# Pacing the late modulation steps of a diffusion transformer block behind its weight loads

## The chip, the cores and the metric

The kernel runs on one core of a Trainium2 chip. The metric is the device time of one execution in microseconds. Five engines work side by side, each through its own instructions in order: TensorE (PE) multiplies, VectorE (DVE) and ScalarE (ACT) do the elementwise work, GpSimd (POOL) and SyncE (SP) here only issue transfers.

## The reference

One block of a diffusion transformer over 256 tokens `x` and 256 context tokens, width 2048, all in float32:

```
mod = silu(c) @ w_ada + b_ada                 # six vectors of 2048: shift, scale, gate, twice
px  = modulate(x, norm1_g, mod 0, mod 1) @ w_in    # and the context likewise
rec = gated linear recurrence, both directions, 8 heads of 128, chunks of 64
att = windowed attention, 8 query heads on 2 key heads, with the context's keys and a sink
mix = (sigmoid(g_r) * (rec @ w_rec) + sigmoid(g_a) * (att @ w_att)) @ w_out
x_mid = x + mod 2 * mix
new_x = x_mid + mod 5 * conv_ffn(modulate(x_mid, norm2_g, mod 3, mod 4))
```

Vectors 0 and 1 are needed at once. The later ones, 2, 4, 3 and 5, are needed behind the merge, and it is their computation that is moved.

## The kernel before

Nearly all the time is matrix products over weights that are read once, 512 KB at a time, in one stream `wst`. A *weight load* (`Stream.load`, L104 to L112) is a transfer from SP's queue into one of four `raw` buffers, a copy on ACT rounded to float32r (`whi`, L109) and a subtraction on DVE that leaves the remainder (`wlo`, L110); three buffers each. Loads are numbered here by their subtraction, 1 to 498. Products are made of two or three matmuls (`hi*hi`, `hi*lo`, `lo*hi`). `duo` (L371) makes two output tiles at once: per load 8 matmuls of 512 columns and 8 of 256. `fold` (L398) empties an output bank: a copy on ACT, an addition on DVE (L400). Five banks serve these outputs (`bankm`), three the small products (`banks`).

The order of stages, with their loads: the first modulation vectors and the first products (1 to 16), q of the recurrence (17 to 32), eight heads of the recurrence with v and the attention's k and v among them (33 to 74), the attention's q (75 to 90), gate g (91 to 106), the recurrent merge gate (107 to 138), the merge (139 to 202; 8 loads for a pair of tiles), the output projection (203 to 234), the FFN. The small products of the recurrence and the attention wait in a list `tasks`; `tick` puts one of them between two pieces of a stage's products.

The late modulation vectors are made on the side, by a generator `ada_steps` (L320). A vector is done in two halves of 16 *steps*; a step issues a transfer of 512 KB from POOL's queue into one of two buffers `araw` (L330) and an accumulation on DVE (L333 the first, L335 the others). After 16 steps come two empty calls, and then one that transposes the sum on PE (L343) and reduces it on DVE (L344): 19 calls for a half, 152 in all. `ada(n)` (L355) makes the next n calls. It is called by hand after pieces of work, 1 to 4 calls together.

A scheduler sets the order on each engine. It goes by the place in the program, moved by hand: a weight load stands up to 60 places early (`LEAD`), a call of `ada` 60 late (`LAG`) and not ahead of the latest load's subtraction. Behind the merge the input is read again into `xm` by two loads of 1 MB (L765, L766), as soon as the recurrence's buffer is free.

Of the kernel before, what the change touches and what calls it, by code (L numbers as in the profile page):

```python
# [50 lines left out]
def block_kernel(ctx, tc, xct, prm, cst, ada2, wst, out):  # L51
# [46 lines left out]
    class Stream:  # L98
        def __init__(self):
            self.half = 0  # L100
            self.pos = 8
            self.hi = self.lo = None

        def load(self, n=8):  # L104
            with tc.high_priority(offset=min(LEAD, max(0, tc.tile_snap_priority() - base[0]))):
                raw, hi, lo = [strm.tile([P, 1024], dt, name=nm, bufs=b)[:, 0:n * P]
                               for nm, dt, b in (("raw", F32, 4), ("whi", F32R, 3), ("wlo", F32R, 3))]
                nc.sync.dma_start(raw, wst[self.half, :, 0:n * P])
                S.copy(hi, raw)  # L109
                self.last = V.tensor_tensor(lo, raw, hi.bitcast(F32), op=ALU.subtract)  # L110
            self.half += 1
            self.hi, self.lo, self.pos = hi, lo, 0  # L112

        def load_raw(self, into):
            with tc.high_priority(offset=min(LEAD, max(0, tc.tile_snap_priority() - base[0]))):
# [10 lines left out]
    st = Stream()  # L126
# [488 lines left out]
    for h in range(H):  # L615
        if h == 4:
            bs = [bank() for _ in range(4)]
            natural(bs, range(4))
            ada(4)
            for tt in range(4):  # L620
                S.copy(vn[:, tt, 512:1024], bs[tt])
        if h == 6:
            bs = [bank() for _ in range(4)]
            natural(bs, range(4))
            ada(4)
            kv_evac(bs)
        for d in range(2):
            if 2 * h + d < 3:
                o = early_f[2 * h + d]
            else:  # L630
                o = bank()
                tform_all(o)
            hgrn_a(h, d, o)
            ada(0 if h > 5 else 2 if h else 1)
        hgrn_q(h)
        tasks += [lambda h=h: hgrn_e(h - 1), lambda h=h: hgrn_b(h), lambda h=h: hgrn_c(h), lambda h=h: hgrn_d(h)]
        ada(1)
        if h == 0:
            q_heads(4)
# [8 lines left out]
    split(kTh, kTl, kT.rearrange("p k (s t) -> p k s t", s=2))  # L648
    split(vah, val, va.rearrange("p (a b) t -> p a b t", a=2))

    bs = [bank() for _ in range(2)]
    for g in range(2):
        if g:
            bs = [bank() for _ in range(2)]
        natural(bs, range(2))
        ada(1)
        if not g:
            assert not tasks
            gr = big.tile([P, KT, T], F32, name="gr", tag="v")
# [54 lines left out]
    for kv in range(2):  # L714
        for blk in range(2):
            tasks += [lambda kv=kv, blk=blk, i=i: att_scores(kv, blk, i) for i in range(4)] + [lambda: None]
            tasks += [lambda kv=kv, blk=blk, k=k: (att_trans(kv, blk, k), att_trans(kv, blk, k + 1)) for k in (0, 2)]
            tasks += [lambda kv=kv, blk=blk: att_out(kv, blk)]
    for h in range(0, H, 2):
        for i, o in enumerate(duo((xx, xx))):  # L720
            fold(qo[:, 0, h + i, :], o)
        ada(2)

    def y_rec(p):
        hs = slice(2 * p, 2 * p + 2)
# [4 lines left out]
    for j in range(0, KT, 2):  # L730
        for i, o in enumerate(duo((xx, xx))):
            fold(gr[:, j + i, :], o)
        if YR <= j < YR + 4:
            assert not tasks
            y_rec(j - YR)
            y_rec(j - YR + 1)
            ada(2)
        else:
            ada(2 + 2 * (j >= 8))
    for j in range(0, KT, 4):  # L740
        S.activation(gr[:, j:j + 4, :], gr[:, j:j + 4, :], AF.Sigmoid)

# [2 lines left out]
    for j in range(0, KT, 2):  # L745
# [6 lines left out]
        for i, ga in enumerate(gas):  # L752
# [4 lines left out]
            V.tensor_tensor(ga[:, 0:T], ga[:, 0:T], ga[:, T:], op=ALU.mult)  # L757
            V.tensor_tensor(ga[:, 0:T], ga[:, 0:T], gr[:, j + i, :], op=ALU.add)
            split(yb[:, j + i, 1, :], yb[:, j + i, 0, :], ga[:, 0:T])
            ada(0 if j + i == 15 else 3 if i else 2)  # L760

    with tc.issue_after(sig.ins):
        S.preload_act_table_set("natural_log_exp_and_others")
    xm = big.tile([P, KT, T], F32, name="xm", tag="qo")
# [24 lines left out]
    for j in range(0, KT, 2):  # L789
        for i, o in enumerate(duo((yb, yb))):  # L790
            with tc.high_priority(offset=RUSH if j == KT - 2 else 0):
                mid_evac(j + i, o)
        if 2 <= j < 8:
            ada(2 if j < 6 else 1)
        if j == 10:
            split(pre[:, 0, :, T:], pre[:, 1, :, T:], sh2[:, :, None].broadcast_to([P, KT, 2]))

# [229 lines left out]
```

## Time and profile before

| | us |
|---|---|
| runs shown: median, lowest, highest | 1717.17, 1711.70, 1721.25 |
| profiled execution, its own time | 1713.84 |
| its span (first to last instruction) | 1712.0 |
| moved, mean rate | 371.84 MB, 217 GB/s |

The page gives each engine's busy time and a chain of what ended last. PE is nearly always busy, but a busy PE need not be at its peak, since the ends of matmuls are modelled. How many matmuls begin in a slice of fixed length tells more, within one stage. Times in the rows are from the span's start.

### The profile page before, as it was taken

The numbers are of one execution on the slowest core, as the hardware profiler recorded it, in microseconds if no ns is written. First come the engines' busy times: TensorE is split into PE (matmuls) and PEld (weight loads), VectorE is DVE, ScalarE is ACT, GpSimd is POOL, SyncE is SP. The second block draws the span as 40 slices with busy tenths as digits, with TensorE's granted clock in tenths as the row PEclk, the third lists the DMA queues.
The fourth block names the chain that finished last, engine by engine and source line by source line (L and its number), as shares of the span: only waits on it lengthen the run. The fifth ranks groups of instructions, "written<-read, shape, count | busy, mean of one in ns | idle before, by whom it ended". The sixth has DMA issues, their size and how long they took to land.

```text
span 1712.0 us, 24746 instructions
## 1 busy us (share of the span) xinstructions
PE 1683.9 (98%) x9438; PEld 1424.6 (83%) x9438; DVE 1202.3 (70%) x1890; ACT 837.2 (49%) x1278; POOL 68.7 (4%) x132
## 2 busy tenths in 40 slices
PE   7999999999999999999999999999999999999999
PEld 2668888888888888888888988888888888888887
DVE  4438876675779787787878788787766655666565
ACT  4237453342646664444454565555555434554332
POOL 0000100100000001010100000000000000000000
PEclk9999999999999999999999999999999999999999
DMA  9986734524346568787866577677655555555564
GB/s 377 385 328 225 259 120 150 198 88 152 104 149 220 173 228 299 253 288 248 301 227 235 184 233 258 222 258 262 219 185 186 190 190 186 193 188 187 193 198 148
DMA packets 104008, 371.84 MB, mean 217 GB/s; under 512 B 11344, under 2 KB 13776, under 8 KB 103888
## 3 DMA queue, kind: packets, MB, share of 16 engines
q1 hardware_dynamic: 85456, 303.14, 50.9%
q0 software_dynamic: 18432, 67.12, 12.3%
q8 instruction: 74, 1.21, 0.3%
q14 instruction: 46, 0.38, 0.1%
HBM read 368.11 MB, written 2.10 MB: 216 GB/s over the span
## 4 chain that ended last, share of the span: by engine, by line
PE 85%; DMA 5%; DVE 5%; issue 3%; ACT 1%; SPq 0%; POOL 0%; DVEq 0%; POOLq 0%; ACTq 0%
PE bankm L68 78%; DMA araw<-in_ada_dram 5%; PE banks L68 5%; DVE wlo L110 1%; DVE acc L335 1%; DMA ringq<-in_wst_dram 1%; DVE xraw L230 0%; ACT whi L109 0%; PE banks L343 0%; PE banks L535 0%; PE banks L701 0%; PE banks L527 0%; SPq L116 0%; ACT t L220 0%; PE banks L536 0%
## 5 line engine op out<-in xcount | busy, mean ns | idle before, releaser
L68 PE MATMUL bankm<-hl,whi 128*128 128x512 f32 (+1 forms) x3392 | 1056.4, 393 | 2.3 <-DVE t L400 2.3
L110 DVE TENSOR_TENSOR wlo<-raw,whi 128x1024 fp32r<-128x1024 f32 x498 | 606.1, 1219 | 297.3 <-ACT whi L109 295.9
L109 ACT CAST whi<-raw 128x1024 fp32r<-128x1024 f32 x498 | 520.3, 1045 | 554.1 <-PE bankm L68 488.2
L68 PEld LDWEIGHTS bankm<-hl,wlo 128*128 128x128 f32 x3104 | 583.8, 188 | 138.6 <-DVE wlo L110 7.1
L68 PE MATMUL bankm<-hl,wlo 128*128 128x256 f32 (+2 forms) x3104 | 665.4, 287 | 4.8 <-DVE wlo L110 4.8
L68 PEld LDWEIGHTS bankm<-hl,whi 128*128 128x128 f32 x3392 | 535.1, 189 | 22.8 <-DVE t L400 3.0
L335 DVE SCALAR_TENSOR_TENSOR acc<-araw,csil,acc 128x1024 f32<-128x1024 f32 x120 | 153.7, 1281 | 37.8 <-DMA araw<-in_ada_dram 37.3
L68 PE MATMUL bankm<-whi,hl 128*128 128x512 f32 x512 | 165.5, 396 | 4.3 <-ACT hl L206 3.3
L68 PEld LDWEIGHTS bankm<-whi,hl 128*128 128x128 f32 x512 | 95.8, 188 | 26.6 <-ACT hl L206 5.5
L330 POOL DMA_DIRECT2D araw<-in_ada_dram x128 | 68.5, 535 | 1144.3 <-DVE acc L335 659.6
L68 PE MATMUL bankm<-wlo,hl 128*128 128x512 f32 x256 | 100.1, 391 | 0.0
L68 PE MATMUL bankm<-yb,whi 128*128 128x512 f32 x256 | 80.8, 397 | 0.0
L68 PE MATMUL bankm<-g,whi 128*128 128x512 f32 x256 | 80.4, 395 | 0.0
L68 PEld LDWEIGHTS bankm<-g,wlo 128*128 128x128 f32 x256 | 48.1, 188 | 11.4
L68 PEld LDWEIGHTS bankm<-yb,wlo 128*128 128x128 f32 x256 | 48.1, 188 | 11.3
L68 PEld LDWEIGHTS bankm<-wlo,hl 128*128 128x128 f32 x256 | 48.1, 188 | 9.5
L852 DVE SCALAR_TENSOR_TENSOR xm<-bankm,modv,xm 128x256 f32<-128x256 f32 x96 | 42.2, 480 | 18.4 <-PE bankm L68 18.3
L834 ACT ACTIVATE fs<-fs,prm 128x256 f32<-128x256 f32 x44 | 26.5, 602 | 55.9 <-DVE fs L400 55.9
L68 PE MATMUL bankm<-yb,wlo 128*128 128x256 f32 x256 | 50.6, 279 | 0.0
L68 PE MATMUL bankm<-g,wlo 128*128 128x256 f32 x256 | 50.3, 278 | 0.0
L195 DVE TENSOR_REDUCE tn<-banks 128x8 f32<-128x32 f32 x8 | 1.5, 192 | 64.7 <-ACT whi L109 51.4
L835 DVE SCALAR_TENSOR_TENSOR fs<-fs,prm,fs 128x255 f32<-128x255 f32 x44 | 21.3, 484 | 26.7 <-ACT fs L834 26.7
(216 smaller groups left out, 1227.5 us busy)
## 6 DMA issues: line engine op xcount, KB each, us to landing
raw<-in_wst_dram SPq DMA_DIRECT2D x490, 512.0 KB, 3.7
araw<-in_ada_dram POOLq DMA_DIRECT2D x128, 512.0 KB, 4.7
ringv<-in_wst_dram SPq DMA_DIRECT2D x24, 512.0 KB, 8.4
ringq<-in_wst_dram SPq DMA_DIRECT2D x20, 512.0 KB, 9.0
araw<-in_wst_dram SPq DMA_DIRECT2D x10, 512.0 KB, 9.3
xraw<-in_xct_dram SPq DMA_DIRECT2D x8, 512.0 KB, 10.2
raw<-in_wst_dram SPq DMA_DIRECT2D x8, 384.0 KB, 8.5
ringkT<-in_wst_dram SPq DMA_DIRECT2D x5, 512.0 KB, 10.1
```

What stands on the lines that cost most here:

```text
L68: return PE.matmul(o, l, r, start=start, stop=stop, skip_group_check=True)
L109: S.copy(hi, raw)
L110: self.last = V.tensor_tensor(lo, raw, hi.bitcast(F32), op=ALU.subtract)
L195: V.tensor_reduce(m8, aps.rearrange("p (q g c) -> p q c g", q=4, g=4)[:, :, 0:2, :], axis=AX.X, op=ALU.add)
L330: nc.gpsimd.dma_start(raw, ada2[idx])
L335: V.scalar_tensor_tensor(acc, raw, csil[:, kt, 0:1], acc, op0=ALU.mult, op1=ALU.add)
L834: S.activation(t, s, AF.Identity, bias=cb[:, f:f + 1], scale=cw[:, f, 1:2])
L835: V.scalar_tensor_tensor(t[:, 1:T], s[:, 0:T - 1], cw[:, f, 0:1], t[:, 1:T], op0=ALU.mult, op1=ALU.add)
L852: V.scalar_tensor_tensor(xm[:, j, :], o[:, T * i:T * i + T], gate2[:, j:j + 1], xm[:, j, :], op0=ALU.mult, op1=ALU.add)
```

## The change

`Stream` gets a rate, `pace`: calls of the generator for 16 loads. Each load adds it to a sum, and whenever the sum reaches 16 one call is made, right behind the load. The rate is 6 from the attention's q on (6 calls over 16 loads), 8 from gate g to the end of the merge (a call every second load), and 0 from there. The calls by hand in these stages go. Heads 6 and 7 of the recurrence get one call for each direction, where they had none, and the output projection two calls after each of four pairs, where it had 2, 2 and 1 after three. The description also names a return of the input in sixteen loads, one per merged tile; the two loads of the input (L769 now) stand as they were.

```diff
@@ Stream.__init__, Stream.load
+            self.pace = self.due = 0
...
             self.hi, self.lo, self.pos = hi, lo, 0
+
+            self.due += self.pace
+            if self.due >= 16:
+                self.due -= 16
+                ada()
@@ heads of the recurrence
             hgrn_a(h, d, o)
-            ada(0 if h > 5 else 2 if h else 1)
+            ada(1 if h > 5 or not h else 2)
@@ attention's q
+    st.pace = 6
     bs = [bank() for _ in range(2)]
...
         natural(bs, range(2))
-        ada(1)
@@ gate g
+    st.pace = 8
     for h in range(0, H, 2):
         for i, o in enumerate(duo((xx, xx))):
             fold(qo[:, 0, h + i, :], o)
-        ada(2)
@@ recurrent merge gate
             y_rec(j - YR + 1)
-            ada(2)
-        else:
-            ada(2 + 2 * (j >= 8))
@@ merge
             split(yb[:, j + i, 1, :], yb[:, j + i, 0, :], ga[:, 0:T])
-            ada(0 if j + i == 15 else 3 if i else 2)
-
+
+    st.pace = 0
@@ output projection
-        if 2 <= j < 8:
-            ada(2 if j < 6 else 1)
+        if 2 <= j < 10:
+            ada(2)
```

In the built order the lines from L115 on are 6 higher than before up to the attention, and 3 higher in the merge and behind it. Three places on DVE show what moves.

The first is the stretch around loads 126 to 135, the end of the recurrent merge gate, in which SP issues the two loads of the input. L335, now L341, is an accumulation. Before, and then with the change:

```order
L335 SCALAR_TENSOR_TENSOR acc<-araw,csil,acc 128x1024
L110 TENSOR_TENSOR wlo<-raw,whi 128x1024 x2
L400 TENSOR_TENSOR gr<-bankm,gr 128x256 x2
L110 TENSOR_TENSOR wlo<-raw,whi 128x1024
L335 SCALAR_TENSOR_TENSOR acc<-araw,csil,acc 128x1024 x2
L110 TENSOR_TENSOR wlo<-raw,whi 128x1024 x2
L335 SCALAR_TENSOR_TENSOR acc<-araw,csil,acc 128x1024 x2
L110 TENSOR_TENSOR wlo<-raw,whi 128x1024
```

```order
L111 TENSOR_TENSOR wlo<-raw,whi 128x1024 x2
L406 TENSOR_TENSOR gr<-bankm,gr 128x256 x2
L111 TENSOR_TENSOR wlo<-raw,whi 128x1024 x4
L406 TENSOR_TENSOR gr<-bankm,gr 128x256 x2
L111 TENSOR_TENSOR wlo<-raw,whi 128x1024 x2
L350 TENSOR_REDUCE modv<-banks 128x4 x2
L339 TENSOR_SCALAR acc<-araw,csil 128x1024
```

The accumulations that stood in twos between the subtractions are gone from here; the reduction of a finished half (L350) and the first accumulation of the next follow behind load 134.

The second is one pair of tiles of the merge, from load 152 on. L400, now L406, is the fold; L755, now L758, the product with the gate.

```order
L110 TENSOR_TENSOR wlo<-raw,whi 128x1024
L335 SCALAR_TENSOR_TENSOR acc<-araw,csil,acc 128x1024 x2
L110 TENSOR_TENSOR wlo<-raw,whi 128x1024
L400 TENSOR_TENSOR t<-bankm,t 128x256 x2
L110 TENSOR_TENSOR wlo<-raw,whi 128x1024
L335 SCALAR_TENSOR_TENSOR acc<-araw,csil,acc 128x1024 x2
L110 TENSOR_TENSOR wlo<-raw,whi 128x1024
L400 TENSOR_TENSOR t<-bankm,t 128x256
L755 TENSOR_TENSOR gr<-gr,t 128x256
```

```order
L341 SCALAR_TENSOR_TENSOR acc<-araw,csil,acc 128x1024
L111 TENSOR_TENSOR wlo<-raw,whi 128x1024
L406 TENSOR_TENSOR t<-bankm,t 128x256 x2
L111 TENSOR_TENSOR wlo<-raw,whi 128x1024
L341 SCALAR_TENSOR_TENSOR acc<-araw,csil,acc 128x1024
L111 TENSOR_TENSOR wlo<-raw,whi 128x1024
L406 TENSOR_TENSOR t<-bankm,t 128x256
L758 TENSOR_TENSOR gr<-gr,t 128x256
```

Two accumulations in a row have become single ones, two subtractions apart.

The third is the front of the attention, loads 96 to 98. L690, now L696, takes the maximum of a row of scores, the start of a softmax. Before, and with the change:

```order
L110 TENSOR_TENSOR wlo<-raw,whi 128x1024
L578 TENSOR_TENSOR gr<-gr,t 128x512
L400 TENSOR_TENSOR qo<-bankm,qo 128x256
L110 TENSOR_TENSOR wlo<-raw,whi 128x1024
L130 TENSOR_TENSOR ab<-banks,ab 128x4x128
L690 TENSOR_REDUCE tn<-banks 128x1 x2
```

```order
L111 TENSOR_TENSOR wlo<-raw,whi 128x1024
L584 TENSOR_TENSOR gr<-gr,t 128x512
L350 TENSOR_REDUCE modv<-banks 128x4 x2
L406 TENSOR_TENSOR qo<-bankm,qo 128x256
L136 TENSOR_TENSOR ab<-banks,ab 128x4x128
L696 TENSOR_REDUCE tn<-banks 128x1
```

Two reductions of a finished half stand here now; before they stood behind load 115.

## The prediction

> **What bounds the kernel now.** I read the page first, then TensorE (PE) in slices, then what released it in the slices that fall short.
>
> ```profile
> PE 1683.9 (98%) x9438; PEld 1424.6 (83%) x9438; DVE 1202.3 (70%) x1890; ACT 837.2 (49%) x1278; POOL 68.7 (4%) x132
> PE 85%; DMA 5%; DVE 5%; issue 3%; ACT 1%; SPq 0%; POOL 0%; DVEq 0%; POOLq 0%; ACTq 0%
> ```
>
> PE is the bound. Nothing in the change takes a matmul away, so all it can win is time in which PE falls behind, and that shows in how many matmuls a slice holds (in brackets), better than in busy time:
>
> ```profile
> core 0: us, PE busy (x) PEld busy (x) DVE busy (x) ACT busy (x) POOL busy (x), PEclk, DMA share, GB/s
> 660.00:680.00 20.00, 17.22 (x90) 14.59 (x90) 13.57 (x14) 6.92 (x9) 2.55 (x5) 0.91 0.99 366
> 680.00:700.00 20.00, 20.00 (x117) 17.43 (x116) 10.31 (x12) 9.84 (x13) 0.09 (x1) 1.00 0.67 229
> 720.00:740.00 20.00, 19.70 (x113) 16.91 (x111) 15.46 (x21) 9.80 (x15) 1.65 (x4) 1.00 0.84 278
> 740.00:760.00 20.00, 18.84 (x108) 16.49 (x109) 18.45 (x26) 10.45 (x17) 2.04 (x4) 1.00 0.84 278
> 820.00:840.00 20.00, 18.88 (x107) 15.75 (x106) 16.67 (x22) 9.45 (x16) 3.17 (x6) 1.00 0.89 310
> 860.00:880.00 20.00, 19.12 (x111) 16.37 (x110) 16.32 (x26) 11.59 (x19) 0.53 (x1) 1.00 0.72 246
> ```
>
> An undisturbed slice holds 117 matmuls, 20/117 = 0.171 us each. The other five lack 27, 4, 9, 10 and 6: 56 x 0.171 = **9.6 us**, of which 4.6 us in the first. All five lie where the change acts. What stopped PE, first in the merge, then in the first slice (VectorE, DVE, runs in order):
>
> ```profile
> 735.20 1.28 DVE L335 SCALAR_TENSOR_TENSOR acc<-araw,csil,acc 128x1024 f32<-128x1024 f32 x1 [1.98 <-DMA araw<-in_ada_dram]
> 738.35 1.28 DVE L335 SCALAR_TENSOR_TENSOR acc<-araw,csil,acc 128x1024 f32<-128x1024 f32 x1 [1.87 <-DMA araw<-in_ada_dram]
> 739.55 1.22 DVE L110 TENSOR_TENSOR wlo<-raw,whi 128x1024 fp32r<-128x1024 f32 x1
> 740.69 0.42 DVE L400 TENSOR_TENSOR t<-bankm,t 128x256 f32<-128x256 f32 x1
> DVE acc L335: 37.3, 32
> ```
>
> In a burst of steps the first two have their weights in the two buffers; the third's transfer starts only when the first step has freed its buffer. DVE then waits for it, and behind it stand the subtraction that makes PE's weights (L110) and the fold that empties PE's bank (L400). The last row is from the view of the transfer's line, under who waited for it: over the whole run DVE stood 37.3 us in 32 waits.
>
> ```profile
> 659.81 0.43 SPq L766 DMA_DIRECT2D xm<-in_xct_dram  x1
> 669.38 1.28 DVE L335 SCALAR_TENSOR_TENSOR acc<-araw,csil,acc 128x1024 f32<-128x1024 f32 x1 [1.20 <-DMA araw<-in_ada_dram]
> 673.42 1.28 DVE L335 SCALAR_TENSOR_TENSOR acc<-araw,csil,acc 128x1024 f32<-128x1024 f32 x1 [2.75 <-DMA araw<-in_ada_dram]
> 674.01 1.05 ACT L109 CAST whi<-raw 128x1024 fp32r<-128x1024 f32 x1 [5.10 <-DMA raw<-in_wst_dram]
> 674.62 1.22 DVE L110 TENSOR_TENSOR wlo<-raw,whi 128x1024 fp32r<-128x1024 f32 x1
> 672.00:676.00 4.00, 1.22 (x7) 1.00 0.87 348
> 676.00:680.00 4.00, 4.00 (x15) 0.57 0.96 318
> 680.00:684.00 4.00, 4.00 (x25) 1.00 0.90 292
> xm<-in_xct_dram SPq DMA_DIRECT2D x2, 1024.0 KB, 11.3
> ```
>
> The same burst, and with it the input's return, two loads of 1 MB (L766). The last three slices are PE alone: it stands 2.78 us, and then runs at a granted clock of 0.57, 15 matmuls instead of 25: 10 x 0.171 = 1.7 us more.
>
> The page "TensorE: Matmul & The Clock Gate" of the Trainium skill (Part 1, What's actually happening) lets the clock fall after an idle window of about 3.4 us; by it a gap of 2.78 us costs no clock, and the sum below would be 1.7 us smaller. The row shows the clock falling, and the measurement decides.
>
> **The change part by part.** The words name a return in sixteen loads; the diff has none, and the built order still has both 1 MB loads, now with one weight load between them instead of two. So only steps are moved. A step issues one 512 KB transfer from POOL's queue and one DVE instruction:
>
> ```profile
> L110 DVE TENSOR_TENSOR wlo<-raw,whi 128x1024 fp32r<-128x1024 f32 x498 | 606.1, 1219 | 297.3 <-ACT whi L109 295.9
> L335 DVE SCALAR_TENSOR_TENSOR acc<-araw,csil,acc 128x1024 f32<-128x1024 f32 x120 | 153.7, 1281 | 37.8 <-DMA araw<-in_ada_dram 37.3
> araw<-in_ada_dram POOLq DMA_DIRECT2D x128, 512.0 KB, 4.7
> DMA to landing us min/median/max: 3.7/4.7/7.8
> ```
>
> From heads 6 and 7 on the calls are, before and after: heads 2 and 6, attention's q 2 and 6, gate g 8 and 8, recurrent gate 20 and 16, merge 37 and 32, output projection 5 and 8, FFN 34 and 32: 108 both times.
>
> *The merge's bursts* (-5.0 us, four slices). A weight load is 16 matmuls, 2.74 us; a step every second load is one per 5.5 us. With two buffers a transfer starts two steps, 11 us, ahead of its use and lands in 4.7. So the waits go. DVE still has to fit: a pair of merged tiles is 8 loads, 21.9 us of PE; DVE has 8 x 1.22 + 14 small operations x 0.42 + 5 steps x 1.28 = 22.1 us before, and with 4 steps 20.8. It was at the brim and is now 5% under. I take all 5.0; the other end is half of it, if a step before a fold still holds a bank.
>
> *The input's return* (-4.6 us). By the order no accumulation stands between that of load 124 and the reduction behind load 134, since two empty calls and the transposes fall there. So DVE has nothing to wait for there, and the POOL queue brings almost nothing beside the 2 MB. What is late next is the raw weights themselves (5.10 us on the ACT row, which came after PE had already stopped). I take the 4.6 gone and charge what is left below; the other end is 2.3.
>
> *What is left* (+1.0 us). Behind the transposes at loads 135 and 172 the held-back steps catch up, about one per load: the third of these is due 5.5 us after the first, its weights 4.7 us after, at worst 7.8. Half a microsecond at each; ends 0 and 3.
>
> *Hgrn of head 7* (+0.9 us). A step now stands on DVE behind the subtraction of load 77, ahead of L467, in a chain on which PE waits already:
>
> ```profile
> 468.93 1.22 DVE L110 TENSOR_TENSOR wlo<-raw,whi 128x1024 fp32r<-128x1024 f32 x1
> 470.62 0.55 DVE L467 TENSOR_SCALAR hb<-hb,lb_t 128x512 f32<-128x512 f32 x1 [0.47 <-ACT hb L466]
> 475.84 0.42 DVE L485 TENSOR_TENSOR hb<-hb,qo 128x256 f32<-128x256 f32 x1
> PEld banks L68: 0.2, 1
> ```
>
> The last row, from the view of L485, is PE's weight load waiting for it. The step fills the 0.47 us of idle and pushes the chain by 1.28 - 0.6 = 0.7; L485 moves ahead of the next subtraction but behind other products, and what PE reads second comes later too. I take 0.9; ends 0 (the moved subtraction gives 1.2 back) and 1.8 (nothing absorbed, one more product).
>
> *The front of the attention* (+0.9, and -0.5 behind it). The order puts seven more accumulations ahead of load 88, ten ahead of load 116, and the two reductions of a finished vector half ahead of load 97 instead of 116.
>
> ```profile
> 480.00:500.00 20.00, 10.47 (x13) 1.00 0.51 161
> 500.00:520.00 20.00, 17.57 (x31) 1.00 0.58 185
> 540.00:560.00 20.00, 20.00 (x36) 1.00 0.74 234
> 550.04 0.48 DVE L696 TENSOR_SCALAR gr<-gr,tn 128x512 f32<-128x512 f32 x1
> 550.58 0.44 PE L701 MATMUL banks<-cst,gr 128*128 128x128 f32 x2
> 796.74 0.69 DVE L344 TENSOR_REDUCE modv<-banks 128x4 f32<-128x512 f32 x1 [0.42 <-PE banks L343]
> ```
>
> The early ones fall into idle time (9.5 us of it from 480 to 500, 2.4 from 500 to 520). Between 540 and 560 DVE has none, and PE's transposes start 0.06 us after the softmax row they read. What comes in ahead of that row: two reductions of 0.69 and 0.2 of small work, less the 0.5 by which an opening step is shorter than the one it replaces: 0.9 after rounding down for the overlap of neighbours. Ends 0 and 3 (if every step that is ahead there, three, counts). In return the same reductions leave the place near 604 where PE waited 0.2, and the fourth block starts with fewer steps ahead of it (0.3).
>
> *The rest* at nothing: the three added calls in the output projection lie where DVE still has 1.4 to 3.2 us of 20 free and PE loses none, and the two that leave the FFN were hidden there.
>
> ```profile
> 900.00:920.00 20.00, 20.00 (x119) 17.49 (x119) 16.77 (x30) 9.65 (x15) 0.53 (x1) 1.00 0.58 186
> 920.00:940.00 20.00, 20.00 (x117) 17.42 (x116) 18.58 (x30) 10.12 (x16) 1.58 (x3) 1.00 0.82 287
> ```
> If that cover were gone, three steps would cost 3.8 us.
>
> Sum: -5.0 - 4.6 + 1.0 + 0.9 + 0.9 - 0.5 = **-7.3 us**. The profiled execution took 1713.84 us (span 1712.0), so 1706.5 on its own scale; it lay 3.3 us below the median of 1717.17, and on the median's scale I get **1710**. The runs shown differ among themselves by 9.5 us, more than the gain.
>
> **The rivals.**
>
> *All of it and more:* the two losses do not appear, and the slower runs of before were slower through these same waits. For it: they hang on when transfers land. Against: PE's edge at 550. -9.6 - 0.5 with nothing lost gives 1707; the 3.3 us on top, 1704.
>
> *The first slice stays:* its stall belongs to the 2 MB, whose sixteen smaller loads are not in the code. For it: the raw weights landed 5.10 us late for ACT. Against: PE stopped on a subtraction behind an accumulation. Then -7.3 + 4.6 = -2.7, 1714.5.
>
> *Slower, DVE becomes the bound in the attention:* ten steps ahead at 1.28 and two reductions are 14.2 us of DVE where 480 to 560 has little idle. It decides from the point at which DVE, once behind, no longer catches up between the blocks. 14.2 - 9.6 = +4.6, and three gaps long enough to cost the clock 1.7 each make +9.7: 1727. Against: seven of the ten fall before 520.
>
> **How the numbers follow.** Forecast 50%, all of it 30%, first slice stays 12%, slower 8%. What this measurement can tell from no change is 0.5%, 8.6 us. A fifth of the forecast (its losses near their lower ends) and all of the second case are beyond it: 0.10 + 0.30 = 0.40 faster. Slower by that much are three quarters of the last, 0.06; the remaining 0.54 is within. The range goes from below 1704 to past 1714.5 with 3 us for the spread of medians: 1702.5 to 1718.
>
> **What would show it.** Right: DVE's wait for the accumulation's transfers falls from 37.3 us to under 20 (what is left lies before 480), the five slices hold 115 to 117 matmuls, the clock stays at 1.00 behind 660, and small new gaps of about 1 us appear near 476 (PE on L491) and 550 (PE on the softmax rows). Wrong: a slice between 500 and 650 that lacks more than 15 matmuls (DVE as bound), a gap of PE near 675 with the raw weights late (the input's return alone), or accumulations that still wait though spaced.

## The result

| | before | with the change |
|---|---|---|
| median, us | 1716.57 (6 runs) | 1705.74 (6 runs, 1704.42 to 1709.57) |
| profiled execution, its own time | 1713.84 | 1707.89 |
| its span | 1712.0 | 1706.1 |

The ratio is 0.9949, with an interval of 0.9932 to 0.9965: 8.8 us faster, within 6.0 to 11.7 us, and the 10.8 us between the two medians lie in it. In two later comparisons, each against its own runs of before, the same kernel had 0.9937 (0.9921 to 0.9953) and 0.9945 (0.9932 to 0.9957), at medians of 1704.51 and 1704.70 us.

The page of the changed kernel has these rows for the engines' busy time and for the chain of waits:

```profile
PE 1681.3 (99%) x9438; PEld 1425.0 (84%) x9438; DVE 1202.3 (70%) x1890; ACT 835.4 (49%) x1278; POOL 69.0 (4%) x132
PE 94%; DVE 3%; DMA 1%; issue 1%; ACT 1%; SPq 0%; DVEq 0%; ACTq 0%
```

PE's own share of the chain went from 85 to 94%; transfers fell from 5 to 1%. PE in slices (busy time, matmuls in brackets, granted clock, DMA share, GB/s), the five that fell short before:

```profile
660.00:680.00 20.00, 20.00 (x119) 1.00 0.77 257
720.00:740.00 20.00, 20.00 (x117) 1.00 0.87 291
740.00:760.00 20.00, 20.00 (x116) 1.00 0.86 277
820.00:840.00 20.00, 20.00 (x117) 1.00 0.85 281
860.00:880.00 20.00, 20.00 (x116) 1.00 0.72 244
```

All are full. The waits that end with a transfer of the accumulation's weights are next: first over the whole run, then from 480 to 1120 us alone (total us, times, longest).

```profile
DVE acc L341 <- DMA araw<-in_ada_dram: 20.7, 19, 2.9
...
DVE acc L341 <- DMA araw<-in_ada_dram: 4.2, 3, 1.8
```

Before, the same stretch had 18 of them:

```profile
DVE acc L335 <- DMA araw<-in_ada_dram: 22.0, 18, 2.8
```

On DVE's timeline, where PE had stood 2.78 us, no accumulation is left, and DVE waits for nothing but the copy on ACT:

```profile
671.44 1.23 DVE L111 TENSOR_TENSOR wlo<-raw,whi 128x1024 fp32r<-128x1024 f32 x1 [1.56 <-ACT whi L110]
...
674.23 1.23 DVE L111 TENSOR_TENSOR wlo<-raw,whi 128x1024 fp32r<-128x1024 f32 x1 [0.89 <-ACT whi L110]
677.06 1.23 DVE L111 TENSOR_TENSOR wlo<-raw,whi 128x1024 fp32r<-128x1024 f32 x1 [1.61 <-ACT whi L110]
```

**Where the time went, to the hundredth.** Every trace has the same 9438 matmuls, so the start of the n-th can be compared between traces. I took the starts of matmuls 1189, 2221, 2473, 3383, 3646, 4735 and 5195; the table gives the time to the first and then between neighbours, in us. The two bold columns are the ones in which the input's return and the merge's bursts lie.

| | to 1189: first products, first heads | to 2221: heads | to 2473: head 7 | to 3383: attention | **to 3646: recurrent gate, input's return** | **to 4735: merge** | to 5195 |
|---|---|---|---|---|---|---|---|
| before | 243.58 | 203.13 | 43.78 | 165.73 | **49.88** | **193.95** | 76.28 |
| the change | 246.99 | 203.12 | 43.93 | 165.66 | **45.27** | **189.21** | 76.28 |
| the change, second profile | 243.41 | 203.13 | 43.93 | 165.64 | **45.27** | **189.21** | 76.27 |
| the change, third profile | 245.21 | 203.13 | 43.93 | 165.59 | **45.27** | **189.21** | 76.27 |

Behind matmul 1189 the change wins 4.61 us at the input's return and 4.74 in the merge, wins 0.07 in the attention, and gives 0.15 back in head 7: -9.27 in all, the same in three executions to 0.1. The rest is before 1189, where the order of the instructions did not change: it took 242.8 to 247.0 us in the eleven profiles with that order (before, the change three times, and seven experiments). The profiled pair shows only -6.0 because this part went 3.4 us against the change. These rows of the changed kernel show it, DVE first, then PE:

```profile
208.95 1.28 DVE L341 SCALAR_TENSOR_TENSOR acc<-araw,csil,acc 128x1024 f32<-128x1024 f32 x1 [1.25 <-DMA araw<-in_ada_dram]
213.14 1.28 DVE L341 SCALAR_TENSOR_TENSOR acc<-araw,csil,acc 128x1024 f32<-128x1024 f32 x1 [2.91 <-DMA araw<-in_ada_dram]
...
223.55 1.74 PE L68 MATMUL banks<-hb 128*128 128x128 f32 x8 [3.70 <-DVE hb L491]
```

In the first heads the accumulations still come in twos; here one waits 2.91 us, and PE waits for a product of the head's chain that DVE reaches late. In the other two profiles of the change PE has no such gap at this place.

### The profile page after: what moved, and what is told of

Read it like the earlier page. It is cut to its first block, busy times and chain, and to the rows that moved or that the text cites. A ratio compares the mean times of both kernels' runs of the same rounds, so it can differ in the third digit from the quotient of the medians.

```text
span 1706.1 us, 24735 instructions
## 1 busy us (share of the span) xinstructions
PE 1681.3 (99%) x9438; PEld 1425.0 (84%) x9438; DVE 1202.3 (70%) x1890; ACT 835.4 (49%) x1278; POOL 69.0 (4%) x132
## 4 chain that ended last, share of the span: by engine, by line
PE 94%; DVE 3%; DMA 1%; issue 1%; ACT 1%; SPq 0%; DVEq 0%; ACTq 0%
PE bankm L68 86%; PE banks L68 5%; DVE wlo L111 1%; DMA araw<-in_ada_dram 1%; DMA ringq<-in_wst_dram 1%; DVE xraw L236 0%; PE banks L541 0%; PE banks L349 0%; PE banks L533 0%; PE banks L707 0%; DVE acc L341 0%; SPq L122 0%; PE banks L542 0%; ACT t L226 0%; PE banks L526 0%
## 5 line engine op out<-in xcount | busy, mean ns | idle before, releaser
L341 DVE SCALAR_TENSOR_TENSOR acc<-araw,csil,acc 128x1024 f32<-128x1024 f32 x120 | 153.5, 1279 | 21.0 <-DMA araw<-in_ada_dram 20.7
L68 PEld LDWEIGHTS bankm<-yb,wlo 128*128 128x128 f32 x256 | 48.1, 188 | 11.3
```

The costliest lines, as they stand in the source:

```text
L68: return PE.matmul(o, l, r, start=start, stop=stop, skip_group_check=True)
L341: V.scalar_tensor_tensor(acc, raw, csil[:, kt, 0:1], acc, op0=ALU.mult, op1=ALU.add)
```

## The experiments

My theory was the prediction's: in a burst the third accumulation is reached before its transfer, DVE stands, PE behind it, and *spacing* the steps cures it. Its rivals: the input's return is the cause of the first slice; DVE's amount of work is the limit; the number of steps in a stage is what counts, not their spacing. In what follows "the gate" and "the merge" are the two bold columns; the floor of each, reached by the change, is 45.27 and 189.21 us. Where an experiment changes the early stages, some small products cross a boundary, and the parts from matmul 1189 to 3383 count together. In three kernels (the recurrent gate alone, and the last two that move the early steps) the gate and the merge hold other matmuls too: a vector's half ends later there, and its eight transposes on PE count in the merge instead of in the gate. With them there, and PE without any gap in either, the two take 45.75 and 188.90 us (Fewer steps early and none in head 7); these are the floors of those three.

### The merge alone

Before's kernel, with the pace only in the merge:

```diff
+    st.pace = 8
     for j in range(0, KT, 2):          # merge
...
-            ada(0 if j + i == 15 else 3 if i else 2)
+    st.pace = 0
...
-        if 2 <= j < 8:
-            ada(2 if j < 6 else 1)
+        if 2 <= j < 10:
+            ada(2)
```

> The kernel before, with the steps paced (one call behind every second weight load) in the merge alone; everything ahead of the merge as before, the output projection's calls as in the change. Theory (in a burst the third accumulation waits for a transfer that the first one's buffer held back, and the weights' subtraction and the bank's fold wait behind it): the four short slices of the merge fill up to 115 to 117 matmuls, the one from 660 to 680 still lacks about 27; 5 us less than before, 1711.6 beside 1716.6. Rival (the gain comes from the steps that were moved ahead of the merge, so that fewer are left in it): with 32 calls as in the change but no earlier steps, the same 5 us would need the counts alone; then the run by hand with the change's counts shows it too. Rival (the input's return is all that matters): 0.

Measured: 1708.71 us, 0.9962 (0.9945 to 0.9978). The gate took 49.36 us, the merge 189.22. The first slice, and DVE in it:

```profile
660.00:680.00 20.00, 17.56 (x93) 0.91 0.98 360
...
669.82 1.29 DVE L341 SCALAR_TENSOR_TENSOR acc<-araw,csil,acc 128x1024 f32<-128x1024 f32 x1 [3.35 <-DMA araw<-in_ada_dram]
672.38 1.29 DVE L341 SCALAR_TENSOR_TENSOR acc<-araw,csil,acc 128x1024 f32<-128x1024 f32 x1 [1.27 <-DMA araw<-in_ada_dram]
```

The two gains are separate: the merge's is had in full without touching the gate, and the gate's stall stays.

### The recurrent gate alone

```diff
+    st.pace = 8
     for j ...                          # recurrent gate
...
-            ada(2)
-        else:
-            ada(2 + 2 * (j >= 8))
+    st.pace = 0
...
-        if 2 <= j < 8:
-            ada(2 if j < 6 else 1)
+        if 2 <= j < 10:
+            ada(2)
```

> The kernel before, with the steps paced in the recurrent merge gate alone (16 calls for 20); the merge keeps its bursts. Theory: the slice from 660 to 680, in which the input returns, fills up (4.6 us) and the clock stays at 1.00; the merge's slices still lack about 29 matmuls together; 4.6 us less, 1712.0. Rival (the slice is short because of the 2 MB of the input, whatever the steps do): 0 to 1 us less, slice still 20 or more short.

Measured: 1711.64 us, 0.9979 (0.9965 to 0.9993). The gate took 45.75 us, its floor with the transposes in the merge, and the merge 193.55, 4.65 over its own. PE in slices, and two accumulations on DVE:

```profile
660.00:680.00 20.00, 20.00 (x116) 1.00 0.94 346
...
740.00:760.00 20.00, 18.72 (x107) 1.00 0.80 286
760.00:780.00 20.00, 19.73 (x112) 1.00 0.87 300
...
840.00:860.00 20.00, 18.80 (x103) 1.00 0.86 314
...
665.59 1.28 DVE L341 SCALAR_TENSOR_TENSOR acc<-araw,csil,acc 128x1024 f32<-128x1024 f32 x1
...
671.16 1.28 DVE L341 SCALAR_TENSOR_TENSOR acc<-araw,csil,acc 128x1024 f32<-128x1024 f32 x1
```

The first slice is full although the input comes back in two loads of 1 MB at a DMA share of 0.94; the merge's stalls stay, a little displaced. In the change no accumulation stands in this place at all, since a half happens to end there. Here they go on, one about every 5.6 us, and none waits: it is the spacing that cures the gate, and not the pause at the half's end alone.

### The input in sixteen loads, without any pace

Before's kernel with what the description names and the diff does not have:

```diff
+    xm = big.tile([P, KT, T], F32, name="xm", tag="qo")
     for j in range(0, KT, 2):          # merge
...
             split(yb[:, j + i, 1, :], yb[:, j + i, 0, :], ga[:, 0:T])
+            nc.sync.dma_start(xm[:, j + i, :], xct[:, j + i, 0:T])
...
-    xm = big.tile([P, KT, T], F32, name="xm", tag="qo")
-    for i in range(2):
-        nc.sync.dma_start(xm[:, 8 * i:8 * i + 8, :], xct[:, 8 * i:8 * i + 8, 0:T])
```

> The kernel before, with the input's return in sixteen loads, one behind each merged tile, as the words of the change describe it; the steps keep their bursts. Theory (burst and return together make the stall of 2.78 us and the slow clock behind it): the wait shrinks to what bursts cost elsewhere, 0 to 1.7 us, so 3 to 4 us less, 1713; the merge's slices stay short by about 29. Rival (the return alone): 4.6 us less and no wait of DVE for a step's transfer near 670. Rival (bursts alone): 0 to 1 us less.

Measured: 1714.70 us, 0.9993 (0.9980 to 1.0006). One of its ten runs, of 9553 us, was not explained; the ratio leaves it out, the median does not (1714.15 us without it). The gate took 47.57 us, 2.31 less than before, and the merge 195.95, 2.00 more. The slices:

```profile
660.00:680.00 20.00, 17.98 (x103) 1.00 1.02 379
...
840.00:860.00 20.00, 18.19 (x105) 1.00 0.82 283
860.00:880.00 20.00, 19.79 (x105) 0.91 0.68 229
```

With the 2 MB gone the first slice lacks 14 matmuls instead of 27, and DVE still waits there for three transfers of the burst (2.18, 1.57 and 1.62 us). The return is therefore not what stops PE: taking it away leaves the stall, while taking the burst away (the experiment before) leaves none of it. Most of the 2.31 us is the clock's: PE stands 2.02 us instead of 2.78, and no slow stretch of the clock follows, which had cost 1.7 us before; in the merge one follows that before did not have (last section). How much the return lengthens the stall, this run does not settle, since PE stood 2.29 us, again without a slow stretch, in another kernel that has before's code there (below). The whole time is unchanged, as far as these runs can tell.

### The input in sixteen loads, on top of the change

The same edit on the changed kernel.

> The changed kernel with the input's return in sixteen loads, one behind each merged tile, so that the change is what its words say. Theory (the return stops nothing once no accumulation waits there): as fast as the change, within 0.1%. Rival (the return in one piece still costs something): 1 to 2 us faster than the change. Third (its 2 MB now lie in the merge and bring waits back there): 1 to 3 us slower than the change, and the merge's slices short.

Measured: 1706.63 us, 0.9944 (0.9924 to 0.9964); gate 45.27, merge 189.21, head 7 43.89. Nothing is left for it to win.

### The change's counts, made by hand in bursts

The changed kernel without its pace; each stage makes as many calls as with it, together:

```diff
-    st.pace = 6
...
         natural(bs, range(2))              # attention's q
+        ada(3)
...
-    st.pace = 8
...
             fold(qo[:, 0, h + i, :], o)    # gate g, each pair
+        ada(2)
...
             y_rec(j - YR + 1)              # recurrent gate, each pair
+        ada(2)
...
             split(yb[:, j + i, 1, :], ...) # merge, each pair
-    st.pace = 0
+        ada(4)
```

> The changed kernel with the same number of calls in every stage, but made by hand together: 3 behind each half of the attention's q, 2 behind each pair of gate g and of the recurrent gate, 4 behind each pair of the merge. Theory (spacing is what counts): the merge's slices stay short, by 15 to 30 matmuls together, and DVE still waits about 30 us for the steps' transfers in the whole run; 1711 to 1715. Rival (counts are what counts, 4 steps a pair in place of 5 take DVE from the brim): as fast as the change, 1705 to 1708, and no short slices.

Measured: 1705.51 us, 0.9947 (0.9930 to 0.9964). Gate 45.27, merge 189.24; attention 166.09, 0.4 more. Waits from 480 to 1120 us:

```profile
DVE acc L341 <- DMA araw<-in_ada_dram: 7.3, 9, 1.9
```

My theory, as I had put it, fell here: without any pace, four calls at once behind each pair of tiles, both gains are there in full. For the gate this says little, since the half ends at the input's return here too and no accumulation stands there; the merge decides. The built order suggests why. W is a subtraction on DVE, A an accumulation, over loads 153 to 160 (a pair of merged tiles):

```
before                    A A W W A A W W A W W W W
the change                A W W A W W A W W A W W
counts made by hand       W W A A W W A W A W W W
```

The scheduler puts a call up to 60 places late, and with four calls for eight loads instead of five it leaves a pair of steps and two single ones, with three loads of pause behind. That the pause is what refills both buffers in time for the next pair is read from this order, not measured.

### The merge paced at its old rate

Before's kernel, the merge paced by 9 (36 calls for 37), nothing else:

```diff
+    st.pace = 9
     for j in range(0, KT, 2):          # merge
...
-            ada(0 if j + i == 15 else 3 if i else 2)
+    st.pace = 0
```

> The kernel before with the merge paced at 9 calls for 16 loads, 36 calls where 37 were made by hand; everything else as before. The run by hand with the change's counts had no short slice, so spacing is not needed once there are 4 calls a pair; this asks whether it is enough with 5. Theory (a third step close behind two others must wait; either fewer or wider apart cures it): the merge's slices at 115 to 117, the one from 660 to 680 short as before, 5 us less. Rival (the number of steps in the merge decides, by what DVE or the transfers can carry): slices short by 15 or more, 0 to 2 us less.

Measured: 1709.36 us, 0.9964 (0.9950 to 0.9978). The merge took 189.25 us, as with the change, at nine calls in 16 loads. So spacing alone is enough too: in the merge DVE accumulates 32 times, as before, and waits 2.8 us for the transfers, in 6 waits, instead of 13.9 us in 12. By hand it is 3.7 us in 6, and with the change none. Either fewer calls or wider spacing will do.

The gate, whose code is before's here, took 47.83 us instead of 49.88. DVE waited the same way in it and PE stood 2.29 us, but the clock held. The rows are PE's timeline, then a slice:

```profile
677.50 0.51 PE L68 MATMUL bankm<-hl,wlo 128*128 128x256 f32 x2 [2.29 <-DVE wlo L111]
...
676.00:680.00 4.00, 2.50 (x15) 1.00 0.83 303
```

### DVE's work kept, the transfers taken away

Before's kernel and its bursts; from step 48 on the accumulations read what lies in their buffers, and no transfer is issued (so the later vectors are not computed):

```diff
-                    raw = strm.tile([P, 1024], F32, name="araw", bufs=2)
...
-                    nc.gpsimd.dma_start(raw, ada2[idx])
+                    if idx < 48:
+                        raw = strm.tile([P, 1024], F32, name="araw", bufs=2)
...
+                        nc.gpsimd.dma_start(raw, ada2[idx])
```

> The kernel before, with its bursts and every accumulation in place, but without the transfers of the steps behind the 48th: those accumulate the last landed weights again, so the four later vectors come out other than the reference's. Theory (PE stops because an accumulation waits for its transfer): no wait from load 104 on, all five slices at 115 to 117, 9 to 11 us less than before. Rival (DVE has too much to do where two accumulations stand together, transfers or not): the merge's slices stay short by 15 or more, at most 5 us less.

Measured: 1704.92 us, 0.9937 (0.9918 to 0.9956). Gate 45.27, merge 189.24. The busy time of PE, PEld, DVE, ACT and POOL from 690 to 880 us, first of before, then of this kernel:

```profile
690.00:880.00 190.00, 186.53 (x1072) 161.53 (x1071) 156.09 (x214) 95.42 (x148) 16.88 (x32) 1.00 0.80 270
```

```profile
690.00:880.00 190.00, 190.00 (x1098) 165.86 (x1097) 162.29 (x222) 97.61 (x152) 0.00 (x0) 1.00 0.55 188
```

DVE does more here than before, still in twos, and PE is not held up once. What stalled PE was waiting, not DVE's work. This kernel also asks less of the DMA engines (a share of 0.55 instead of 0.80), so it does not by itself part the wait for the accumulation's transfers from a lack of bandwidth; the change, the counts by hand and the paced merge show that the stalls go with the transfers in place.

### The early stages too

The part before matmul 1189 still waits, and differently each time. Here no steps stand in the recurrence's q and the first two heads; from behind head 1 they are paced by 18 to the end of the heads, and by 8 in the attention's q:

```diff
-            ada(2)                         # recurrence's q
...
-            ada(4)                         # v, and the attention's k and v
...
-            ada(4)
...
-            ada(1 if h > 5 or not h else 2)
...
+        if h == 1:
+            st.pace = 18
...
-        ada(1)                             # each head
...
-    st.pace = 6
+    st.pace = 8
```

> The changed kernel, with the steps taken out of the recurrence's q and its first two heads and paced by 18 for 16 loads from head 1 to the end of the heads, 8 from the attention's q on. In all profiles so far PE loses 3 to 6 us between 160 and 225 us, where bursts of steps still stand and DVE waits 7 to 8 us for their transfers. Theory (the same waits): that stretch loses 1 to 2 us, and the run is 2 to 4 us faster than the change, 1701 to 1704 beside 1715. Rival (these gaps belong to the first heads' own chain between DVE and ACT): the gaps stay, no difference from the change.

Measured: 1706.66 us, 0.9956 (0.9939 to 0.9973), no faster than the change. Matmul 1189 starts at 237.86 us, 5 to 9 earlier, but head 7 takes 46.67 instead of 43.93. DVE and then PE there:

```profile
463.19 1.28 DVE L341 SCALAR_TENSOR_TENSOR acc<-araw,csil,acc 128x1024 f32<-128x1024 f32 x1 [1.67 <-DMA araw<-in_ada_dram]
...
466.66 1.28 DVE L341 SCALAR_TENSOR_TENSOR acc<-araw,csil,acc 128x1024 f32<-128x1024 f32 x1
467.86 0.54 DVE L472 TENSOR_SCALAR hb<-hb,lb_t 128x512 f32<-128x512 f32 x1
...
473.75 1.11 PE L68 MATMUL banks<-hb 128*128 128x128 f32 x4 [2.85 <-DVE hb L490]
```

The accumulations stand ahead of head 7's chain, which PE waits for at once. The runs reach from 1703.24 us, which is the profiled one, to 1712.47, so more than this gap varies; what, one profile cannot show.

### Fewer steps early and none in head 7

The changed kernel, with fewer calls in q and heads 0 and 1, none in heads 0, 6 and 7, the four with v and the four with k and v paced over their 8 loads, and the rates raised where PE had room (8 in the attention's q, 10 in the gate, 9 in the merge):

```diff
-            ada(2)
+            ada(1 if h0 else 0)            # recurrence's q
...
+            st.pace = 8                    # v; the same for the attention's k and v
             natural(bs, range(4))
-            ada(4)
+            st.pace = 0
...
-            ada(1 if h > 5 or not h else 2)
+            ada(0 if not h or h > 5 else 1 if h == 1 else 2)
...
-        ada(1)
+        ada(1 if 0 < h < 6 else 0)
...
-    st.pace = 6
+    st.pace = 8
...
+    st.pace = 10                           # recurrent gate
...
+    st.pace = 9                            # merge
...
-        if 2 <= j < 10:
+        if j < 10:
```

> The changed kernel with fewer steps where the recurrence's chain between DVE and PE is on the edge: none in the first four heads of q and in heads 0, 6 and 7, one for each call around head 1, the naturals of the heads paced (4 calls over 8 loads); what is left out comes later, the recurrent gate paced by 10, the merge by 9, two calls more in the output projection. The run with the early stages paced closed the gaps between 160 and 225 us, and opened one of 3.1 us at 470 where held-back steps met head 7. Theory (these gaps are steps that wait or stand in the chain of a head): both stretches without gaps over 1 us, 2 to 4 us faster than the change beside it. Rival (the merge and the recurrent gate at the fuller rates wait again, and take it back): short slices between 640 and 880, no faster than the change.

Measured: 1706.51 us, 0.9951 (0.9933 to 0.9968), a miss: no faster than the change measured beside it (1704.51). Head 7 is back at 43.78, but matmul 1189 is still at 244.60: the longest gap of PE in the chains of the first heads has moved to 233 us, with another of 1.06 us behind it.

```profile
234.91 0.49 PE L68 MATMUL banks<-hb 128*128 128x128 f32 x2 [1.54 <-DVE hb L543]
```

The rival, that PE waits again in the gate and the merge at the fuller rates, did not come true: they take 45.75 and 188.90 us, without a gap of PE.

### Early pace, head 7 free

The steps paced by 16 from behind head 1 to the last products of v and k, none in heads 6 and 7, and the rates of the last experiment behind:

```diff
-            ada(2)                         # recurrence's q
...
-            ada(4)                         # v, and the attention's k and v
...
-            ada(4)
+            st.pace = 0                    # behind k and v, head 6
...
-            ada(1 if h > 5 or not h else 2)
...
+        if h == 1:
+            st.pace = 16
...
-        ada(1)                             # each head
...
-    st.pace = 6
+    st.pace = 8
...
+    st.pace = 10                           # recurrent gate
...
+    st.pace = 9                            # merge
...
-        if 2 <= j < 10:
+        if j < 10:
```

> The kernel with the early stages paced, mended: steps begin behind head 1, one call behind every weight load up to the v and k products of head 6, none in heads 6 and 7, and what is left out comes later (recurrent gate paced by 10, merge by 9, ten calls in the output projection). Theory (PE's gaps are steps in the way of a head's chain): from 160 to 240 us PE loses about 1 us instead of 6 to 9, no gap near 470, nothing short behind 480; 4 to 6 us faster than the change beside it, about 1700. Rival (whatever is taken from one chain lands in the next): a new gap of 2 us or more elsewhere, within 2 us of the change.

Measured: **1702.05 us** (1700.16 to 1703.34), 0.9927 (0.9913 to 0.9940); the change beside it 1704.70 (1703.03 to 1706.14). Its median is the lowest of the study, by 2.65 us against the change, less than the 4 to 6 that I had expected; the runs of the two hardly overlap, but the intervals of their ratios do. Matmul 1189 is at 238.02 and head 7 at 43.78, but the gate takes 47.17 (1.42 over its floor) and the merge 191.15 (2.25 over). The steps that were taken out early come back there, but their rate alone is not the reason, since the kernel of the last experiment has the same rates and loses nothing there. In the merge an accumulation waits 2.55 us for its transfer, and behind it DVE works without a pause until PE stands at 878; the rows are DVE's, then PE's:

```profile
863.98 1.28 DVE L341 SCALAR_TENSOR_TENSOR acc<-araw,csil,acc 128x1024 f32<-128x1024 f32 x1 [2.55 <-DMA araw<-in_ada_dram]
...
876.23 1.28 DVE L341 SCALAR_TENSOR_TENSOR acc<-araw,csil,acc 128x1024 f32<-128x1024 f32 x1
877.43 1.21 DVE L111 TENSOR_TENSOR wlo<-raw,whi 128x1024 fp32r<-128x1024 f32 x1
878.57 0.41 DVE L136 TENSOR_TENSOR yb<-t,yb 128x256 fp32r<-128x256 f32 x1
...
879.03 0.74 PE L68 MATMUL bankm<-yb,whi 128*128 128x512 f32 x2 [1.06 <-DVE yb L136]
```

In the gate it is the raw weights that come late beside the input's return: ACT waits 3.55 us for them at 672. Why PE stands for late transfers in this kernel and not in that of the last experiment, the two profiles do not show.

### The change again, twice

> The changed kernel as it is, beside the next one and the kernel before on one chip. Both theories: 8 to 10 us less than before, 0.994 to 0.996; in its profile gaps of 2 to 5 us between 160 and 225 us, none of more than 1 us behind.

> The changed kernel once more, beside the next one and the kernel before on one chip: 0.993 to 0.996 of the kernel before.

Measured: 1704.51 and 1704.70 us, ratios as above. Behind matmul 1189 the three profiles agree to 0.1 us; before it they differ by 3.6 us. PE's gap there moves: 3.70 us near 220 in the first profile, none there in the others; near 183 it waited 1.07 us in the first, and in the second and third:

```profile
183.43 0.49 PE L68 MATMUL banks<-hb 128*128 128x128 f32 x2 [1.45 <-DVE hb L543]
```

```profile
184.07 0.49 PE L68 MATMUL banks<-hb 128*128 128x128 f32 x2 [2.69 <-DVE hb L543]
```

## Why the prediction was right, and where it was not

The forecast was 1710 us, in a range of 1702.5 to 1718, and the measured 1705.74 lies in it. By steps:

**What bounds the kernel: right.** The five short slices are full, as "115 to 117 matmuls" and "clock 1.00 behind 660" had it. The waits for the accumulation's transfers fell from 37.3 to 20.7 us, a little short of "under 20", and 16.5 us of what is left lie before 480.

**The two gains: right in size.** The input's return was put at -4.6 and measured -4.61; the merge's bursts at -5.0 and -4.74. The kernels with one of the two show them apart (49.36 and 189.22, 45.75 and 193.55). That the first agrees to the hundredth is luck in part: forecast and measurement are both read against the same profile of before, in which a slow stretch of the clock cost 1.7 us behind the stall. In the merge paced at its old rate the same code of the gate met no such stretch and took 47.83 us; against that execution the cure is worth 2.56.

**Their reason: half right.** The transfers' waits are the cause, as the run without transfers shows. But the spacing, which I gave as the cure, is one of two: the counts of the change without its pace win as much. And the budget that put DVE "at the brim", 22.1 of 21.9 us (its terms add up to 22.0), was wrong. I had added durations, 27 rows for a pair of tiles; but a DVE row begins before the one ahead of it ends: 719.77 + 1.23 is 721.00, and the next starts at 720.91, as DVE's timeline of the changed kernel shows.

```profile
719.77 1.23 DVE L111 TENSOR_TENSOR wlo<-raw,whi 128x1024 fp32r<-128x1024 f32 x1 [0.22 <-ACT whi L110]
720.91 0.42 DVE L136 TENSOR_TENSOR yb<-t,yb 128x256 fp32r<-128x256 f32 x1
721.25 0.42 DVE L406 TENSOR_TENSOR t<-bankm,t 128x256 f32<-128x256 f32 x1
```

Some 0.08 us for each, 2.2 for the 27, and the row of before quoted above has 214 instructions in 190 us, 24.7 for a pair. The busy view says it at once: 156.09 of 190, 82%. These 190 us hold the end of the gate too, but from 706 to 900 us it is no more than 162.57 of 194, 84%, so DVE had room in the merge even before. As the run without transfers shows, what made it late was that it stood still in the waits.

**The three losses: mis-sized, all too high.** "What is left" was +1.0 and is 0: gate and merge reach the same floor as without transfers (45.27 and 189.24). Hgrn of head 7 was +0.9 and is +0.15. The new gap at L491 is there, where I had expected it, but the two that before had in this chain, 0.10 and 0.05 us, closed; where the rest of its 0.54 us was won back is not shown:

```profile
480.38 1.10 PE L68 MATMUL banks<-hb 128*128 128x128 f32 x8 [0.54 <-DVE hb L491]
```

The front of the attention was +0.9 with -0.5 behind it, and the whole stretch comes out at -0.07. An accumulation stands right ahead of the softmax row, as foreseen, but PE had other products until then, and its transposes start 0.05 us behind the row's end, as they did before (0.06):

```profile
553.71 1.27 DVE L341 SCALAR_TENSOR_TENSOR acc<-araw,csil,acc 128x1024 f32<-128x1024 f32 x1
554.90 0.48 DVE L702 TENSOR_SCALAR gr<-gr,tn 128x512 f32<-128x512 f32 x1
...
555.43 0.44 PE L707 MATMUL banks<-cst,gr 128*128 128x128 f32 x2
```

The mistake is the same in both: I charged a delay on DVE to PE in full from one row of small slack, while in these stretches a chain's other products leave some.

**The sum and its scale.** The terms gave -7.3 and the part behind matmul 1189 measured -9.27; the difference of 2.0 is those three losses (2.3 us with the 0.5 taken off, where 0.1 was measured) less the 0.26 by which the merge won less than I took. The other 2.3 us of the forecast's 4.3 come from putting it "on the median's scale": I added the 3.3 us by which the profiled execution lay under the median of three runs. The medians of before in the later comparisons were 1714.4 to 1715.0, close to the profile's 1713.84. The first 245 us account for up to 4.2 us of such a difference.

**The rivals.** "All of it and more" was nearer than the forecast: its first condition, that the losses do not appear, came true to 0.15 us, and it gave 1707 or 1704. Its second, that the slower runs of before were slower through these waits, was not tried, since none of them was profiled. "First slice stays" fell by the run with the pace in the gate alone, where the 2 MB stayed and the slice was full. "DVE becomes the bound in the attention" fell with that stretch at 165.66 us for 165.73. And the description's sixteen loads, which the diff lacks, brought nothing that these runs can tell from noise, with the pace or without.

**What stays open.** What the return of the input adds to the gate's stall (PE stood 2.78, 2.44 and 2.29 us in three profiles with it, 2.02 in the one without); whether a third buffer, which no run had, would do as much as the spacing; why the first 245 us differ by 4.2 us between executions of one order (the waits of the accumulations there differ, but what makes a transfer late was not tried); and a kernel that has all floors at once. The fastest kernel's 238.0 us to matmul 1189, and behind it the lowest that other kernels showed (412.6 to matmul 3383, then 45.27, 189.21, 76.3 and 735.6), add up to a span near 1697 us, an estimate of what the order of the steps could still bring; the fastest kernel has 1701.4. The clock goes with the time of the first 245 us: the four of the eleven profiles in which it did not fall between 150 and 245 us took 242.8 to 243.5, the five in which it fell for one window of 3.41 us 243.4 to 247.0, and the two in which it fell for two 245.2 and 245.7.

## What to carry to other kernels

A side stream with two buffers is paid for by whatever stands behind it on the engine that consumes it: count how far apart its uses come on that engine, against the time from a freed buffer to a landed transfer (here 4.7 us at the median, and up to 7.8), and ask this of the built order, since a scheduler may spread a burst or make one. An engine's load is the busy view's, not a sum of durations. And where two traces have the same number of instructions on the bound engine, compare the starts of the n-th: here it gave each stage's gain to 0.1 us, where whole executions of one kernel differ by up to 10 us. The matmuls between two such marks must be the same ones in both traces; eight transposes that cross a mark shift it here by half a microsecond.

## What was not expected of the hardware

**The clock falls after short gaps, but not after every one.** In the kernel with sixteen loads PE stood twice for 2.02 us. The rows are PE's timeline, then stretches of 3.41 us (busy, matmuls, granted clock, DMA share, GB/s):

```profile
674.89 0.51 PE L68 MATMUL bankm<-hl,wlo 128*128 128x256 f32 x2 [2.02 <-DVE wlo L110]
...
860.21 0.50 PE L68 MATMUL bankm<-hl,wlo 128*128 128x256 f32 x2 [2.02 <-DVE wlo L110]
```

```profile
669.71:673.13 3.42, 3.16 (x18) 1.00 1.03 407
673.13:676.54 3.41, 1.65 (x10) 1.00 1.06 381
676.54:679.95 3.41, 3.41 (x22) 1.00 0.99 388
...
857.45:860.86 3.41, 1.39 (x9) 1.00 0.49 156
860.86:864.27 3.41, 3.41 (x13) 0.50 0.94 323
```

After the first the clock held; after the second it was at 0.50 for 3.41 us, 13 matmuls instead of 22. The difference is where the gap lies. In every trace here the changes of the clock are whole multiples of 3.41 us apart (in the kernel before it fell at 184.81 and at 676.33 us, 144 times 3.413 apart), so it seems to be set window by window, and the stretches above are such windows. The first gap lies across a bound, with 0.26 us in one window and 1.76 in the next; the second lies whole in one. In the fourteen traces, from 15 to 1640 us, all 20 windows at full clock in which PE was idle for 1.78 us or more were followed by a slow one, and none in which it was idle for 1.77 or less. So a gap of 2 us costs 2 us or nearly 4, by where it falls; how much of the spread of times this makes was not tried. The page "TensorE: Matmul & The Clock Gate" of the Trainium skill (Part 1, What's actually happening) puts the fall behind an idle window of about 3.4 us; here a window of that length that was idle for 1.78 us of it was enough, and the measurement decides. The same section says that the window runs freely and not from the start of the work; the traces agree, since the spacing is 3.41 us in all of them, but the bounds lie at another distance from the span's start in each (0.49 us past a multiple of it in the kernel before, 1.97 in the changed one).

**Equal transfers of one queue landed at very different times.** The two loads of the input, 1 MB each, landed in a median of 11.3 us before and of 6.6 with the change, at the same size and from the same queue. In the slice from 660 to 680 us the DMA engines were busy for 0.99 of the time before and 0.77 with the change, which would fit that the other transfers under way made the difference; no run here parts the two:

```profile
xm<-in_xct_dram SPq DMA_DIRECT2D x2, 1024.0 KB, 6.6
```
